# Hybrid decoder layer on one core: other chunks for the down projection, weights asked for in portions, a spread head, a convolution in steps and one load on another queue

## The chip, the cores and the metric

The kernel runs on one core of a Trainium2 chip. The metric is the device time of one launch in microseconds (us), median over the runs. A core has TensorE (PE, matrix products into PSUM), VectorE (DVE), ScalarE (ACT), GpSimd (POOL) and SyncE (SP); each works through its own instructions in order, and SP and POOL also issue DMA transfers, each in the order of its own queue.

## The reference

One decoder layer on an input `x` of 1024 positions by 1024 features, in float32, one sequence:

```python
x = x + 0.5 * swiglu(rms_norm(x, g1), gate1, up1, down1)          # d_ff = 2816
h = rms_norm(x, g_mix)
z = h @ w_in + b_in               # q, k, v of attention; q, k, v, gates of an mLSTM; two branch gates
y_attn  = sliding_window_attention(a_q, a_k, a_v, sinks) @ w_proj_attn      # 16 heads, window 128
qk      = silu(causal_depthwise_conv(concat(m_q, m_k), w_conv))             # width 4
y_mlstm = (sigmoid(m_o) * head_norm(mlstm(qk, m_v, m_i, m_f))) @ w_proj_mlstm
x = x + (sigmoid(g_a) * y_attn + sigmoid(g_m) * y_mlstm) @ w_out
x = x + 0.5 * swiglu(rms_norm(x, g2), gate2, up2, down2)
out = rms_norm(x, g_final)

def swiglu(x, gate, up, down): return (silu(x @ gate) * (x @ up)) @ down
def rms_norm(x, g): return x * rsqrt(mean(x * x) + 1e-6) * g
```

## The kernel before, in words

Positions lie along the free axis in two halves of 512, features along the partitions in eight tiles of 128, so `X[k][h]` is a tile of 128 x 512 in float32. Each float32 product is made of three TensorE matmuls: an operand is split into a high part, rounded for TensorE by a ScalarE copy, and a low part, the rest, by a VectorE subtraction (`parted`: lines 346 and 347). Then high times high, high times low and low times high are summed in PSUM.

**Feed-forward.** Both feed-forwards use a scheme of seven products for a 2 x 2 block product, numbered `PRODUCTS = 1, 2, 6, 7, 5, 4, 3`, with sums of weight blocks (`sum_of`) and sums of activation blocks (`mixed`) formed on VectorE beforehand. `gate_up` walks over eleven slices of the hidden features. Its `load` fetches a weight block of 128 x 1024 over SP's queue, `split` makes high and low parts, `product` does the matmuls (line 437), and `group` reads the result from PSUM (line 476 is ScalarE's copy for product 1). The first `LEAD` = 4 slices do products 1 and 2 ahead of the others, while the remaining operands are still being made; their blocks are loaded again for products 6 to 3, at fixed counts of `done` prepared units. The results are multiplied (`gated`), combined into the seven operands of the down product (`paired`) and stored to DRAM as the array `gd`.

The down stage, in `ffn`, cuts the eleven slices into chunks, `DOWN = ((0, 3), (3, 4), (7, 4))` as (first, count). Over each chunk it runs seven steps, one for each product, in the order `DOWN_ORDER = 1, 2, 6, 7, 4, 5, 3`. A step is four groups (`times`, matmuls at line 656) of 3 matmuls for each slice, 512 columns wide; the last step of the second feed-forward is done in two halves of 256 columns. What comes in:

- the chunk's weights, four blocks, over SP's queue (`load`): those of the first chunk all at product 2 of the last gate/up slice (`tail`), those of a later one in the chunk before;
- the step's operand from `gd`, over GpSimd's queue, three steps ahead (`fetch`): one in `tail` at product 7, three more at product 4, and from step 1 on one at each step;
- the rows of `x` to which the result is added (`loadx`, SP's queue): even tiles of the first half ahead of the first step, the rest in steps 1 to 3.

`prepare` makes high and low parts of the coming weights, two units a step, somewhat over one step ahead, and forms the weight sums behind them. Lines 688 to 694 are VectorE's additions of results to `u` and to the rows of `x`. The additions, the low parts and the sums stand in one order on VectorE.

**Head.** The kernel loads `x`, takes squares on ScalarE and adds them on VectorE (`stats`, lines 261 and 264; an addition is held back until the next square is issued), makes row sums with small matmuls against a constant (`rstd_rows`, line 272), the root on GpSimd, and spreads the row factor `r` over the partitions (`spread`, ScalarE copy at line 282). Before, all eight squares of the second half stand in ScalarE's order ahead of the copy of the first half's `r`; VectorE then normalises (line 752) and the products of the first gate/up stage start.

**Mix.** Each half goes through `mix`. Attention and mLSTM blocks are issued in a hand-made order, and between them `fill` takes steps of matrix products (`gemm`) from a list of tasks, as many as make up the time given. `ensure` runs tasks to their end where a result is needed. `gemm` hands its PSUM result to an evaluator; for the tiles of the convolution it is `ev_conv`, which does the four taps at once on VectorE (line 955) and defers only the silu (`later`: ScalarE's tanh at line 960, VectorE at line 961). `out_b` at line 1137 is the addition that makes an attention output, `ot`, from the PSUM tile `po`.

**Residual.** After the first half's mix, eight products with `w_out` are added to rows of `x` from DRAM (`xload` over SP's queue, two rows ahead, `ev_res` at line 1436), squared and summed. The norm of the second half runs beside it, its eight rows loaded over SP's queue just before.

**End.** The last step of the second feed-forward closes each tile with `done2`, and `final` multiplies the last quarter by its row factor (line 1550) and stores it.

Of the kernel before, what the change touches and what calls it, by code (L numbers as in the profile page):

```python
# [13 lines left out]
AF = mybir.ActivationFunctionType  # L14
# [5 lines left out]
KT = D // 128  # L20
# [3 lines left out]
HALVES = ((0, HS), (HS, HS))  # L24
QUARTERS = ((HS, HS // 2), (HS + HS // 2, HS // 2))
UNIT = D
DOWN = ((0, 3), (3, 4), (7, 4))
DOWN_ORDER = (1, 2, 6, 7, 4, 5, 3)
RING = 24
PRODUCTS = (1, 2, 6, 7, 5, 4, 3)  # L30
# [75 lines left out]
def layer(ctx, tc, I, out):  # L106
# [159 lines left out]
    def rstd_rows(psum, acc, v, n=4):  # L266

        flush()
        ps = psum.tile([128, n, 2], F32, name="mm")
        for b in range(n):  # L270
            for j, a in enumerate(acc):
                nc.tensor.matmul(ps[:, b], a[:, 128 * b:128 * b + 128], mean, start=j == 0, stop=j == len(acc) - 1)
        nc.vector.tensor_scalar(v, ps[:, :, 0], EPS, None, op0=OP.add)
        nc.gpsimd.tensor_tensor(v, v, mhalf[:, :n], op=OP.pow)

# [115 lines left out]
    def gate_up(n, pool, psum, op, gd, lead, tail, ahead):  # L391
# [131 lines left out]
        def prepare():  # L523

            nonlocal done
            nxt = next(rest, None)
            if nxt is None:
                yield from ahead()
                return
            lo = split(*nxt)  # L530
            yield
            lo()
            done += 1
            if done == 3:
                load(3, 0, 0), load(3, 0, 1)
                early.clear()
            elif done == 4:
                load(0, 1, 0), load(0, 1, 1)
            elif done == 7:
                load(0, 0, 1)  # L540
            elif done == 8:
                load(0, 0, 0), load(1, 0, 0)
                sum_of(0, 3), sum_of(0, 2)
            behind(*nxt)
            yield
# [17 lines left out]

    def ffn(n, pool, psum, op, gd, X, loadx, lead, done):

        steps = [(c, p) for c in range(len(DOWN)) for p in DOWN_ORDER]
        units = [(c, p, j) for c, p in steps for j in range(2)]
        last = len(DOWN) - 1
# [23 lines left out]

        def sum_of(c, j, i):
            w = 256 * DOWN[c][1]
            a, b, d, e = (raw[c, m, h][:, w * j:w * j + w] for m in range(2) for h in range(2))
            if i == 2:
                two_sum[c, j] = pool.tile([128, UNIT], F32, name="wr", bufs=4)[:, :w]
            t = two_sum.get((c, j))
            f, o, x, y = {3: (nc.vector.tensor_sub, a, a, d), 2: (nc.vector.tensor_sub, t, e, a),
                          1: (nc.vector.tensor_add, d, d, e), 4: (nc.vector.tensor_sub, b, b, t)}[i]  # L600
            f(o, x, y)

        def prepare():
            nonlocal ready
# [23 lines left out]
        def tail(p):  # L628
            if p == 2:
                for m in range(2):  # L630
                    for h in range(2):
                        load(0, m, h)
            elif p == 7:
                moving["buf", 0] = slot(1, [2, 4, 2, HS])
                fetch(0)
            elif p == 4:
                moving["buf", 1] = slot(2, [2, 4, 2, HS])
                for i in range(1, 4):
                    fetch(i)

        yield from gate_up(n, pool, psum, op, gd, lead, tail, prepare)
# [16 lines left out]
            return ps  # L658

        for i, (c, p) in enumerate(steps):  # L660
            if i:
                fetch(i + 3)
            if i == 1:
                for d in range(0, KT, 2):
                    loadx(d, 1)
# [40 lines left out]
    with ExitStack() as c1:  # L706
# [12 lines left out]
            nc.sync.dma_start(X[k][h], I["x"][h, :, k])  # L719

        def lead():
            yield from mixed(pool, X, 0, r1, op, own)
            bg.append(late_consts(pool))

        def warm(n):
# [10 lines left out]
        acc = [temp(pool) for h in range(2)]  # L736
        for k in range(KT):
            stats(pool, acc[0], X[k][0], k == 0)
        rs0, rs1 = (rstd_of(pool, psum, [a]) for a in acc)
        next(rs0)  # L740
        warm(12)
        for k in range(KT):
            stats(pool, acc[1], X[k][1], k == 0)
        for r in rs0:
            pass
        next(rs1)
        warm(4)
        next(f1)
        for k in range(KT + 1):
            o = op[1 + k // 4] if k < KT else None  # L750
            if k < KT:
                nc.vector.scalar_tensor_tensor(X[k][0], X[k][0], gains[:, 0, k:k + 1], r, op0=OP.mult, op1=OP.mult)
                nc.scalar.activation(o(k % 4, 0), X[k][0], AF.Copy)
            if k:
                j, o = k - 1, op[1 + (k - 1) // 4]
                nc.vector.tensor_sub(o(j % 4, 1), X[j][0], o(j % 4, 0).bitcast(F32))
            if k == 3:
                for r1 in rs1:
                    pass
        Hm = []  # L760

        def done1(d, p):
# [38 lines left out]
    def gemm(key, src, ev):  # L801
        hi, lo = W.get(key)
        ps = psum.tile([128, HS], F32, name="mm")
        for k in range(KT):
            mm3(ps, hi[:, k], lo[:, k], src[:, k, 0], src[:, k, 1], k == 0, k == KT - 1)
            if k == 3:
                W.mid()
            if k in (1, 3, 5):
                yield 1.3
        later = ev(ps)  # L810
        yield 1.3
        if later:
            deferred.append(later)


    deferred = []
# [1 line left out]
    def mix(hf, sH, sO, sQ, H, m0):  # L818
# [3 lines left out]
        def step():  # L822
            if state["cur"] is None:
                if not queue:
                    return None
                key, g = queue.pop(0)
                state["cur"] = (key, g)
            try:
                t = next(state["cur"][1])
                while t and deferred:  # L830
                    deferred.pop(0)()
                pump()
                return t
            except StopIteration:
                done.add(state["cur"][0])
                state["cur"] = None
                return 0.0
# [106 lines left out]
        def ev_conv(kind, t, dst):  # L944
            tile_ = (T_MQ if kind == 0 else T_MK) + t
            w = conv[:, 4 * kind + t]
            hs = hist[:, 4 * kind + t]

            def ev(ps):
                z = pool.tile([128, 3 + HS], F32, name="zb", bufs=1)  # L950
                nc.gpsimd.tensor_copy(z[:, :3], hs)
                nc.scalar.activation(z[:, 3:], ps, AF.Identity, bias=binf[:, tile_:tile_ + 1])
                nc.vector.tensor_scalar(dst, z[:, 0:HS], w[:, 0:1], None, op0=OP.mult)
                for j in range(1, 4):
                    nc.vector.scalar_tensor_tensor(dst, z[:, j:j + HS], w[:, j:j + 1], dst, op0=OP.mult, op1=OP.add)
                nc.gpsimd.tensor_copy(hs, z[:, HS:])

                def later():
                    th = z[:, :HS]
                    nc.scalar.activation(th, dst, AF.Tanh, scale=0.5)  # L960
                    nc.vector.scalar_tensor_tensor(dst, th, 1.0, dst, op0=OP.add, op1=OP.mult)
                return later
            return ev


# [452 lines left out]
    with ExitStack() as c3:  # L1418
# [10 lines left out]
        def xload(d):  # L1429
            if d < KT:  # L1430
                xr[d] = op.tile([128, HS], F32, name="xr", bufs=4)
                nc.sync.dma_start(xr[d], xd[0, :, d])

        def ev_res(d):
            def ev(ps):
# [189 lines left out]
```

## Time and profile before

| | |
|---|---|
| runs | 2423.58, 2416.15, 2421.65 us; median 2421.65 |
| profiled execution | 2410.58 us, its span 2408.4 us |
| mean granted TensorE clock | 0.988 |
| TensorE busy | 2341.1 us (97%), 11138 matmuls |
| VectorE busy | 1700.8 us (71%) |
| ScalarE busy | 971.1 us (40%) |
| GpSimd busy | 240.8 us (10%) |
| DMA | 361.46 MB, mean 150 GB/s |

The profile is of one execution, with times counted from its first instruction. Busy times are sums over an engine's instructions; waits are the idle time of an engine ahead of an instruction, put down to the work that ended last before it. L437 is line 437 of the kernel. The granted clock is a share of TensorE's full clock.

### The profile page before, as it was taken

To read this page: it belongs to the slowest core of one execution; us is meant where nothing else is said; L and a number is where in the kernel's file an instruction comes from. 1 tells how busy PE (TensorE), PEld (TensorE's weight loads), DVE (VectorE), ACT (ScalarE), POOL (GpSimd) and SP (SyncE) were. 2 spreads that over 40 slices of the span, in tenths; PEclk is the share of its full clock that TensorE was granted. 3 is DMA by queue.
4 is the path that set the end of the run, shared out by engine and by line. 5 is a ranking of instruction groups with operands and counts; after the bars stand their busy time and mean duration, and the time that the engine had idled before them with its cause. 6 is when DMAs were issued, how large, how long until landed. Compare 5 with 4: busy or idle time off the path is not lost.

```text
span 2408.4 us, 30172 instructions
## 1 busy us (share of the span) xinstructions
PE 2341.1 (97%) x11138; PEld 1947.2 (81%) x11138; DVE 1700.8 (71%) x2720; ACT 971.1 (40%) x1728; POOL 240.8 (10%) x242
## 2 busy tenths in 40 slices
PE   8999999999999999999999999999999999999997
PEld 7788888878887878888777878888888888887886
DVE  7998877866667754555567754554689988887766
ACT  5434343322247742333347742333353433332223
POOL 0000000000034220100044220100000000000000
PEclk9999999999999999999999999999999999999999
DMA  4464543998431223222532223222545645359862
GB/s 171 130 203 166 164 148 133 337 334 281 166 106 53 75 64 99 69 80 84 176 94 60 67 66 98 66 82 88 183 147 162 200 147 182 124 206 393 281 212 104
DMA packets 154324, 361.46 MB, mean 150 GB/s; under 512 B 13504, under 2 KB 22848, under 8 KB 154176
## 3 DMA queue, kind: packets, MB, share of 16 engines
q1 hardware_dynamic: 131728, 277.79, 35.4%
q0 software_dynamic: 21584, 81.53, 9.8%
q8 instruction: 88, 1.44, 0.2%
q14 instruction: 60, 0.49, 0.1%
q10 hardware_dynamic: 864, 0.21, 0.1%
HBM read 263.27 MB, written 96.21 MB: 149 GB/s over the span
## 4 chain that ended last, share of the span: by engine, by line
PE 77%; DVE 11%; DMA 6%; ACT 3%; issue 2%; SPq 0%; POOL 0%; DVEq 0%; ACTq 0%
PE mm L437 30%; PE mm L656 13%; PE mm L327 8%; PE mm L329 8%; PE mm L328 8%; DMA gd<-nsq 2%; PE mm L936 1%; PE mm L937 1%; PE mm L938 1%; DMA nsq<-x 1%; DMA s<-dn 1%; DVE wlo L347 1%; ACT P L1085 1%; DVE P L1075 1%; PE lm L1220 1%
## 5 line engine op out<-in xcount | busy, mean ns | idle before, releaser
L437 PE MATMUL mm<-s,whi 128*128 128x512 f32 x2112 | 653.7, 391 | 5.4 <-ACT nsq L476 4.9
L437 PEld LDWEIGHTS mm<-s,whi 128*128 128x128 f32 x2112 | 397.7, 188 | 90.5 <-ACT nsq L476 5.8
L327 PE MATMUL mm<-s,whi 128*128 128x512 f32 x1056 | 422.9, 400 | 0.9 <-DVE s L1405 0.9
L329 PE MATMUL mm<-s,wlo 128*128 128x512 f32 x1056 | 414.7, 393 | 1.5 <-POOL wlo L88 1.5
L328 PE MATMUL mm<-s,whi 128*128 128x512 f32 x1056 | 413.8, 392 | 0.0
L437 PE MATMUL mm<-s,wlo 128*128 128x512 f32 x1056 | 412.1, 390 | 0.0
L656 PE MATMUL mm<-s,whi 128*128 128x512 f32 (+1 forms) x1264 | 385.6, 387 | 2.8 <-DVE nsq L694 1.5
L656 PEld LDWEIGHTS mm<-s,whi 128*128 128x128 f32 x1264 | 237.1, 190 | 51.8 <-DVE nsq L694 2.4
L656 PE MATMUL mm<-s,wlo 128*128 128x512 f32 (+1 forms) x632 | 245.0, 388 | 7.3 <-DVE wlo L347 7.3
L329 PEld LDWEIGHTS mm<-s,wlo 128*128 128x128 f32 x1056 | 199.5, 189 | 46.5 <-POOL wlo L88 3.2
L327 PEld LDWEIGHTS mm<-s,whi 128*128 128x128 f32 x1056 | 199.9, 189 | 42.4 <-issue 4.1
L437 PEld LDWEIGHTS mm<-s,wlo 128*128 128x128 f32 x1056 | 198.9, 188 | 41.1 <-DVE wlo L347 0.2
L328 PEld LDWEIGHTS mm<-s,whi 128*128 128x128 f32 x1056 | 199.9, 189 | 37.5
L88 DVE TENSOR_TENSOR wlo<-wraw,whi 128x1024 fp32r<-128x1024 f32 (+1 forms) x138 | 174.6, 1265 | 68.1 <-ACT whi L76 67.7
L76 ACT ACTIVATE whi<-wraw 128x1024 fp32r<-128x1024 f32 (+1 forms) x154 | 159.4, 1042 | 68.8 <-DMA wraw<-win 19.7
L346 ACT ACTIVATE whi<-wr 128x1024 fp32r<-128x1024 f32 (+1 forms) x122 | 127.9, 1049 | 100.2 <-DVE wr L427 50.2
L346 ACT ACTIVATE whi<-s 128x1024 fp32r<-128x1024 f32 (+1 forms) x72 | 70.9, 987 | 211.5 <-PE mm L656 191.8
L347 DVE TENSOR_TENSOR wlo<-wr,whi 128x1024 fp32r<-128x1024 f32 (+1 forms) x122 | 147.5, 1209 | 8.1 <-ACT whi L346 8.0
L346 ACT ACTIVATE nsq<-nsq 128x512 fp32r<-128x512 f32 x162 | 98.9, 624 | 134.3 <-DVE nsq L347 55.4
L656 PEld LDWEIGHTS mm<-s,wlo 128*128 128x128 f32 x632 | 119.9, 190 | 32.6 <-DVE wlo L347 9.0
L590 POOL DMA_DIRECT2D s<-gd x42 | 31.9, 760 | 1109.5 <-DMA s<-dn 439.3
L485 DVE TENSOR_TENSOR nsq<-mm,nsq 128x512 f32<-128x512 f32 x132 | 90.4, 685 | 59.1 <-PE mm L437 59.0
(277 smaller groups left out, 3452.8 us busy)
## 6 DMA issues: line engine op xcount, KB each, us to landing
gd<-nsq SPq DMA_DIRECT2D x308, 256.0 KB, 4.4
s<-gd POOLq DMA_DIRECT2D x28, 2048.0 KB, 8.4
wraw<-win SPq DMA_DIRECT2D x84, 512.0 KB, 3.6
wr<-gu SPq DMA_DIRECT2D x74, 512.0 KB, 4.6
s<-gd POOLq DMA_DIRECT2D x14, 1536.0 KB, 12.7
s<-dn SPq DMA_DIRECT2D x16, 1024.0 KB, 9.7
wraw<-gu SPq DMA_DIRECT2D x30, 512.0 KB, 4.2
nsq<-x SPq DMA_DIRECT2D x32, 256.0 KB, 7.2
```

The lines of the kernel that those rows point to most:

```text
L76: self.nc.scalar.activation(hv, v, AF.Copy)
L88: (self.nc.gpsimd if self.on_pool else self.nc.vector).tensor_sub(lv, v, hv.bitcast(F32))
L327: nc.tensor.matmul(ps, hi, xh, start=first, stop=False)
L328: nc.tensor.matmul(ps, hi, xl, start=False, stop=False)
L329: nc.tensor.matmul(ps, lo, xh, start=False, stop=last)
L346: nc.scalar.activation(hi, x, AF.Copy)
L347: return lambda: nc.vector.tensor_sub(lo, x, hi.bitcast(F32))
L437: nc.tensor.matmul(ps, a[:, k], op[p](k, x), start=first and k == 0 and j == 0, stop=k == 3 and j == 2, skip_group_check=not first)
L485: nc.vector.tensor_add(st[s, to, w], ps, st[s, key, w])
L590: nc.gpsimd.dma_start(t, gd[PRODUCTS.index(p), s0:s0 + a].rearrange("s p i t -> p s i t"))
L656: nc.tensor.matmul(ps, wt[:, f], t[:, f, x, c], start=first and f == 0 and q == 0, stop=f == a - 1 and q == 2, skip_group_check=not first)
L936: nc.tensor.matmul(ps, x[:, 0], hi, start=k == 0, stop=False)
```

## The change

- The down stage's chunks become 4, 3, 4 slices in the first feed-forward and 4, 4, 3 in the second. The first chunk's four weight blocks are asked for at products 2 (two), 6 and 5 of the last gate/up slice. `fetch` runs at every step from step 0 on, with two instead of three in `tail` at product 4. `sum_of` in the down stage picks its blocks only as it uses them.
- In `gate_up`, block `(0, 0, 0)` is loaded again after six prepared units instead of eight.
- In the head, the first weights' parts are made earlier; two squares of the second half stand ahead of the copy of `r`, the other six stand between the normalising steps, each in a tile of its own, and are not added on VectorE: `rstd_rows` sums the seven tiles on TensorE, with its loops exchanged. The second half's `r` is waited for in `lead`.
- A convolution's three later taps and its last multiply become four deferred steps, one at each step of the list of tasks; an evaluator of a convolution first runs all that is still deferred. The tanh is issued behind the third tap.
- `xload` issues over GpSimd's queue.

```diff
-DOWN = ((0, 3), (3, 4), (7, 4))
+CHUNKS = {1: ((0, 4), (4, 3), (7, 4)), 2: ((0, 4), (4, 4), (8, 3))}
...
         ps = psum.tile([128, n, 2], F32, name="mm")
-        for b in range(n):
-            for j, a in enumerate(acc):
-                nc.tensor.matmul(ps[:, b], a[:, 128 * b:128 * b + 128], mean, start=j == 0, stop=j == len(acc) - 1)
+        for j, a in enumerate(acc):
+            for b in range(n):
+                nc.tensor.matmul(ps[:, b], a[:, 128 * b:128 * b + 128], mean, start=j == b == 0,
+                                 stop=j == len(acc) - 1 and b == n - 1, skip_group_check=True)
...
             elif done == 4:
                 load(0, 1, 0), load(0, 1, 1)
+            elif done == 6:
+                load(0, 0, 0)
             elif done == 7:
                 load(0, 0, 1)
             elif done == 8:
-                load(0, 0, 0), load(1, 0, 0)
+                load(1, 0, 0)
                 sum_of(0, 3), sum_of(0, 2)
...
         def tail(p):
             if p == 2:
                 for m in range(2):
-                    for h in range(2):
-                        load(0, m, h)
+                    load(0, m, 0)
+            elif p == 6:
+                load(0, 1, 1)
+            elif p == 5:
+                load(0, 0, 1)
             elif p == 7:
                 moving["buf", 0] = slot(1, [2, 4, 2, HS])
                 fetch(0)
             elif p == 4:
                 moving["buf", 1] = slot(2, [2, 4, 2, HS])
-                for i in range(1, 4):
+                for i in range(1, 3):
                     fetch(i)
...
         for i, (c, p) in enumerate(steps):
-            if i:
-                fetch(i + 3)
+            fetch(i + 3)
...
         def lead():
-            yield from mixed(pool, X, 0, r1, op, own)
+            for r in rs1:
+                yield
+            yield from mixed(pool, X, 0, r, op, own)
...
-        rs0, rs1 = (rstd_of(pool, psum, [a]) for a in acc)
+        rs0 = rstd_of(pool, psum, [acc[0]])
         next(rs0)
-        warm(12)
-        for k in range(KT):
+        warm(4)
+        next(f1)
+        for k in range(2):
             stats(pool, acc[1], X[k][1], k == 0)
+        flush()
         for r in rs0:
             pass
-        next(rs1)
-        warm(4)
-        next(f1)
+        warm(8)
+        squares = [acc[1]]
+        rs1 = rstd_of(pool, psum, squares)
         for k in range(KT + 1):
...
-            if k == 3:
-                for r1 in rs1:
-                    pass
+            if k < KT - 2:
+                squares.append(temp(pool))
+                nc.scalar.activation(squares[-1], X[2 + k][1], AF.Square)
+            elif k == KT - 2:
+                next(rs1)
...
         later = ev(ps)
         yield 1.3
-        if later:
-            deferred.append(later)
+        deferred.extend(later or [])
...
-                while t and deferred:
+                if t and deferred:
                     deferred.pop(0)()
...
             def ev(ps):
+                while deferred:
+                    deferred.pop(0)()
                 z = pool.tile([128, 3 + HS], F32, name="zb", bufs=1)
...
-                for j in range(1, 4):
+
+                def tap(j):
                     nc.vector.scalar_tensor_tensor(dst, z[:, j:j + HS], w[:, j:j + 1], dst, op0=OP.mult, op1=OP.add)
-                nc.gpsimd.tensor_copy(hs, z[:, HS:])
-
-                def later():
-                    th = z[:, :HS]
-                    nc.scalar.activation(th, dst, AF.Tanh, scale=0.5)
-                    nc.vector.scalar_tensor_tensor(dst, th, 1.0, dst, op0=OP.add, op1=OP.mult)
-                return later
+                    if j == 3:
+                        nc.gpsimd.tensor_copy(hs, z[:, HS:])
+                        nc.scalar.activation(z[:, :HS], dst, AF.Tanh, scale=0.5)
+
+                def last():
+                    nc.vector.scalar_tensor_tensor(dst, z[:, :HS], 1.0, dst, op0=OP.add, op1=OP.mult)
+                return [lambda j=j: tap(j) for j in range(1, 4)] + [last]
...
                 xr[d] = op.tile([128, HS], F32, name="xr", bufs=4)
-                nc.sync.dma_start(xr[d], xd[0, :, d])
+                nc.gpsimd.dma_start(xr[d], xd[0, :, d])
```

## Rows read from the trace of the kernel before

**Rows 1.** The page: span, and busy time, share and instructions of each engine.
```profile
span 2408.4 us, 30172 instructions
...
PE 2341.1 (97%) x11138; PEld 1947.2 (81%) x11138; DVE 1700.8 (71%) x2720; ACT 971.1 (40%) x1728; POOL 240.8 (10%) x242
```

**Rows 2.** Waits of PE: instruction <- releaser: total us, times, longest us.
```profile
PE mm L656 <- DVE wlo L347: 7.3, 4, 2.2
...
PE mm L437 <- ACT nsq L476: 4.9, 2, 4.8
...
PE po L1126 <- DVE ot L1137: 4.3, 4, 2.0
PE mm L272 <- DVE nacc L264: 3.9, 1, 3.9
```

**Rows 3.** Stretches: us; PE, PEld, DVE, ACT, POOL busy; granted clock; DMA share; GB/s.
```profile
200.00:400.00 200.00, 200.00 (x884) 165.67 (x883) 164.35 (x214) 79.69 (x107) 0.00 (x0) 1.00 0.49 158
60.00:80.00 20.00, 15.25 (x62) 12.06 (x61) 18.50 (x25) 13.23 (x23) 0.35 (x1) 0.91 0.25 74
430.00:490.00 60.00, 60.00 (x266) 49.71 (x265) 47.08 (x66) 20.29 (x30) 6.38 (x8) 1.00 1.07 381
485.00:525.00 40.00, 34.77 (x142) 27.28 (x141) 28.02 (x39) 7.38 (x8) 3.00 (x4) 0.96 1.07 387
845.00:865.00 20.00, 17.48 (x82) 13.91 (x81) 15.90 (x29) 12.34 (x29) 9.31 (x12) 0.91 0.18 55
...
2200.00:2240.00 40.00, 35.13 (x145) 27.68 (x144) 28.86 (x40) 7.71 (x9) 3.00 (x4) 0.96 1.08 392
```

**Rows 4.** Timeline of the head: start us, us, engine, line, op, count, [idle <- releaser].
```profile
12.36 0.95 PE L272 MATMUL mm<-mean,nsq 128*128 128x2 f32 x8
...
19.66 0.58 ACT L282 ACTIVATE nsq<-mm 128x512 f32<-128x512 f32 x1
20.95 1.84 PE L272 MATMUL mm<-mean,nsq 128*128 128x2 f32 x8 [4.42 <-DVE nsq L264]
...
25.19 1.40 DVE L752 SCALAR_TENSOR_TENSOR nsq<-nsq,gains 128x512 f32<-128x512 f32 x2
...
26.64 1.52 PE L437 MATMUL mm<-s,whi 128*128 128x512 f32 x2 [0.47 <-ACT s L753]
```

**Rows 5.** Timeline of the first gate/up stage, VectorE and ScalarE near 70 us.
```profile
68.51 1.23 DVE L427 TENSOR_TENSOR wraw<-wraw,wr 128x1024 f32<-128x1024 f32 x1 [1.03 <-DMA wraw<-gu]
...
71.03 1.06 ACT L346 ACTIVATE whi<-wr 128x1024 fp32r<-128x1024 f32 x1 [6.77 <-DVE wr L427]
```

**Rows 6.** Timeline of the first down stage: its first matmul, and VectorE at 492 us.
```profile
454.88 0.62 PE L656 MATMUL mm<-s,whi 128*128 128x512 f32 x2
...
492.16 0.69 DVE L690 TENSOR_TENSOR nsq<-nsq 128x512 f32<-128x512 f32 x1 [4.92 <-DMA nsq<-x]
492.77 0.95 DVE L347 TENSOR_TENSOR wlo<-s,whi 128x768 fp32r<-128x768 f32 x1
```

**Rows 7.** Timeline of VectorE at the end of the first attention stage.
```profile
853.35 3.48 DVE L955 SCALAR_TENSOR_TENSOR lq<-zb,conv,lq 128x512 f32<-128x512 f32 x3
...
857.61 0.69 DVE L961 SCALAR_TENSOR_TENSOR lq<-zb,lq 128x512 f32<-128x512 f32 x1 [0.78 <-ACT zb L960]
858.23 0.68 DVE L1137 TENSOR_TENSOR ot<-po,ot 64x512 f32<-64x512 f32 x1
```

**Rows 8.** Timeline of VectorE in the residual stage.
```profile
1173.60 0.69 DVE L1436 SCALAR_TENSOR_TENSOR xr<-mm,xr 128x512 f32<-128x512 f32 x1 [5.12 <-DMA xr<-xd]
...
1190.06 0.68 DVE L1436 SCALAR_TENSOR_TENSOR xr<-mm,xr 128x512 f32<-128x512 f32 x1
...
1192.11 0.68 DVE L264 TENSOR_TENSOR nacc<-nacc,nsq 128x512 f32<-128x512 f32 x1
```

**Rows 9.** Timeline of VectorE in the tail: first final multiply, last addition of results.
```profile
2385.78 0.75 DVE L1550 SCALAR_TENSOR_TENSOR nsq<-nsq,gains 128x512 f32<-128x512 f32 x1 [1.18 <-ACT nsq L282]
...
2394.16 0.42 DVE L694 TENSOR_TENSOR nsq<-mm,nsq 128x256 f32<-128x256 f32 x1
```

More of the change, by code (lines that the diff above doesn't have):

```diff
@@ L564, in ffn @@
     def ffn(n, pool, psum, op, gd, X, loadx, lead, done):
+        DOWN = CHUNKS[n]
         steps = [(c, p) for c in range(len(DOWN)) for p in DOWN_ORDER]
@@ L594, in sum_of, with at @@
             w = 256 * DOWN[c][1]
-            a, b, d, e = (raw[c, m, h][:, w * j:w * j + w] for m in range(2) for h in range(2))
+            def at(m, h):
+                return two_sum[c, j] if m == 2 else raw[c, m, h][:, w * j:w * j + w]
             if i == 2:
                 two_sum[c, j] = pool.tile([128, UNIT], F32, name="wr", bufs=4)[:, :w]
[L598 to L601, printed above, removed]
+            f, o, x, y = {3: (nc.vector.tensor_sub, (0, 0), (0, 0), (1, 0)), 2: (nc.vector.tensor_sub, (2, 0), (1, 1), (0, 0)),
+                          1: (nc.vector.tensor_add, (1, 0), (1, 0), (1, 1)), 4: (nc.vector.tensor_sub, (0, 1), (0, 1), (2, 0))}[i]
+            f(at(*o), at(*x), at(*y))
         def prepare():
```

## The prediction

> **What bounds the kernel now.** The page comes first: TensorE's matmuls are busy 97% of a span of 2408.4 us [rows 1]. No other engine is near that on average, so only stretches in which TensorE stands still, or runs at half clock, can be won. A busy matmul row doesn't show throughput, so the table by stretches is read next, for counts: in 200 us without a stall it has 884 matmuls of 512 columns, 0.2262 us each [rows 3]. Any other stretch of such matmuls has lost its length minus count times 0.2262:
> - 60 to 80 us, first gate/up stage: 62 matmuls are 14.0 us of work, **6.0 us lost** [rows 3].
> - 485 to 525 us, first down stage: 142 are 32.1 us, **7.9 us lost** [rows 3].
> - 2200 to 2240 us, second down stage: 145 are 32.8 us, **7.2 us lost** [rows 3].
>
> The ends of the two attention stages have small shapes too, so there idle time and clock are read: 17.48 us busy of 20 (2.5 us idle) at a mean granted clock of 0.91, that is 1.8 us more at the lower of the two levels, **4.3 us** [rows 3]. The row of the second, 1390 to 1410 us, has the same two numbers, so 8.6 us together.
>
> The list of TensorE's waits says who ended them [rows 2]: the down stages wait for the low parts of weights from VectorE (7.3 us), the gate/up stage for a PSUM copy by ScalarE (4.8 us), attention for VectorE's `ot` (4.3 us), and the residual stage once for the last add of squares (3.9 us). The timeline then shows what is late behind each of them. All of these are places that the diff touches.
>
> **Part 1, head and first gate/up stage.** Before, VectorE starts normalising the first half at 25.19 us, since ScalarE's copy of the first `r` (19.66) stands behind all squares of the second half, and VectorE first adds seven of these [rows 4]. Now ScalarE does two squares ahead of that copy and VectorE one add; six adds (0.68 us each, as the L264 row shows [rows 8]) become row sums on TensorE. I work out VectorE's new order: the first half's row sums are done at 13.3 us as before [rows 4], two low parts of weights (1.23 us each, as the L427 row, which has their operation and shape [rows 5]) and one add bring 16.6 or somewhat later, then come eight steps of a multiply and a low part, 0.7 us each [rows 4], against a start at 25.19. But the second half's row sums grow from 8 to 56 small matmuls, and stand in TensorE's order ahead of the first product. Eight of them took 1.84 us at 20.95, after an idle gap, and 0.95 us at 12.36, behind the warm-up [rows 4]. 56 at the first rate are 12.9 us and, from about 17.4 us (16.6 and a square), end at 28.5 to 30 us; at the second they are 6.7 us, so they follow ScalarE's squares and end near 26. So the first product starts between 26.5 and 30 us against 26.64 [rows 4], and VectorE, which has one row-sum result in its loop to wait for, is 4.9 to 7.5 us ahead of before. I take the slow side, since the new ones too come piecemeal behind squares, with gaps: start +0.7 us, VectorE 4.9 us ahead.
>
> Of the clock in this head the rows show 8 row-sum records in 1.84 us after an idle gap of 4.42 us [rows 4]. The Trainium skill ("TensorE: Matmul & The Clock Gate", Part 1) says that an idle engine drops to half rate and that sustained activity releases it; were the row sums to count as activity, the products would start at full rate and part 1 would give some 3 us more, which is inside the range below.
>
> The 6.0 us at 60 to 80: TensorE waits for the ScalarE copy at L476, which is queued behind a weight copy that sat 6.77 us until VectorE had formed a weight sum (L427), which itself had waited only 1.03 us for the reload of `(0, 0, 0)` [rows 5]. So earlier loading alone buys 1.0 us; the rest of the stall is VectorE's lateness. With both, the copy comes 4.9 + 1.0 = 5.9 us earlier, which is more than the wait of 4.8 [rows 2]; the stall goes. Part 1: -6.0 + 0.7 = **-5.3** (from -9, fast row sums, to -1, if VectorE's lead is used up). In the second feed-forward the same earlier load meets no wait of TensorE: 0.
>
> **Part 2, down chunks and portioned loads.** In 430 to 490 us the DMA engines move 381 GB/s at a share over 1 [rows 3]: full. VectorE's residual add at L690 waits 4.92 us for a reloaded row of `x`, the low part of a weight is queued behind it (492.77), and TensorE waits for that [rows 6]. The chunk starts at 454.88 [rows 6]. A step has 36 matmuls with 3 tiles, 48 with 4: 8.14 or 10.86 us. That add belongs to step 3 after its first 9 (12) matmuls: due at 481.3 before, landed 492.1, so 10.8 us late, and the weight behind it is due at step 4's half, 454.9 + 4.5 x 8.14 = 491.5. Now the add is due at 490.2 and the weight at 503.8. Bytes up to that row, by the shapes: before 4 x 0.79 (weights) + 24 x 0.26 (products' rows) + 7 x 1.57 (fetches) + 9 x 0.26 (`x`) = 22.7 MB from 430 to 492, in fair agreement with the 381 GB/s. Now 4 x 1.05 + 6.3 + 6 x 2.1 + 2.4 = 25.5 MB, 67 us at 381: landing at 497. Plus an add and a low part (0.69 + 1.2) the weight is ready at 499, 5 us in hand. So the loss goes, in both feed-forwards. The upper bound is 7.9 + 7.2 = 15.1; I leave 3 us for what remains, more in the second, whose next chunk is 4 tiles too and so loads 4.2 MB instead of 3.1: **-12** (-15 to 0). The portions: the last of the first four weights is now asked for after product 5, two products (2 x 24 x 0.2262 = 10.9 us) ahead of the first step; if it is late by a few us, ScalarE waits, and it is busy 40% [rows 1].
>
> The price is at the end: the second feed-forward's last chunk now has 3 tiles. VectorE works from 2385.78 to 2394.58 (8.8 us) without a gap, on adds and on eight final multiplies [rows 9], past the last matmul. In the last step TensorE has 72 instead of 96 half-width matmuls, 24 x 0.113 (half of 0.2262) = 2.7 us less cover, and the multiplies start 1 us earlier, as the groups ahead of them are shorter: **+2** (0 to +4).
>
> **Part 3, convolution in steps.** VectorE does three taps in one piece of 3.48 us, then waits for ScalarE's tanh, then does L961 at 857.61, and only then the `ot` that TensorE waits for [rows 7]. Spread over steps of the filler, one tap of 1.16 us stands ahead of `ot`, which can start at 853.35 + 1.16 = 854.5 instead of 858.23; as the longest of the four waits for it was 2.0 us [rows 2], 856.2 is soon enough. The stall goes at the end of both attention stages; later heads are pulled in by an ensure that runs all taps at once, as before, and TensorE isn't short there. Of 8.6 us I take **-6.5** (-8.6 to -2).
>
> **Part 4, residual rows on GpSimd's queue.** The first row stood on the SP queue behind eight loads, and VectorE waited 5.12 us for it [rows 8]. That delay mostly heals by itself: the last add of squares ends at 1192.79, and TensorE's wait of 3.9 us [rows 2] with it, so the product ahead ended at 1188.9, and the chain of the last rows starts at 1190.06, only 1.1 us behind it [rows 8]. So -1 (-1.5 to 0). GpSimd's queue then holds eight DMA issues ahead of or between the norm's work; the waits of the last four are for stores two steps old. The Trainium skill ("Trainium Kernel Development and Optimization", Key Constraints) says that all queues share the same DMA engines and another issuer only saves issue time; by it this part would give 0, and the 5.12 us agree only in that they were order, not bandwidth.
>
> **Sum**: -5.3 - 12 + 2 - 6.5 - 1 = -22.8. The profiled execution took 2410.58 us (2.2 around its span), so the new one should take about 2388. The median of the runs shown is 2421.65, 11 us above the profiled one; taking the same difference, the forecast is 2421.65 - 22.8 = **2399**.
>
> **The rivals.**
> - *The row of transfers still ends the down stages.* If SP's queue is served a third of the rate while fetches are pending, the row of `x` lands a few us later than 499, and the later ones and the next chunk's weights too. For: the engines stay full, and fetches are a third larger. Against: 5 us in hand. Part 2 then gives -3 instead of -12: 2408.
> - *Row sums and spread taps don't pay.* VectorE stays as late at the first weight sum, or `ot` stays behind two taps: parts 1 and 3 at their poor ends, +4.3 and +4.5: also 2408.
> - *All stalls go and the row sums are quick*: -9 - 15 - 8.6 - 1.5 + 1 = -33: 2389.
> - *Slower: fetches late.* Four fetches of 2.1 MB instead of 1.57 are asked for around the start of each down stage. If they are served behind the weights, each step's operand lands after its step begins. The second fetch must land within 15.7 us of its issue at about 450; 2.1 MB at a third of 381 GB/s is 16.5 us a fetch, against a step of 10.86: 5.7 us lost a step, over six steps in two stages +68, and 2421.65 - 10.8 + 68 = 2479. It decides from 2 us a step (24 us). Against it: no wait of TensorE for a fetch among the first ones listed, in stages already full.
>
> **Chances.** Forecast (2394 to 2405): 0.45. All go (below 2394): 0.16. The two partial cases (2405 to 2414): 0.21. Within 0.3% (7 us, about what a measurement here can tell from nothing): 0.10, where both partial cases come together. Slower: 0.08. So faster 0.82. The range from 2387 to 2415 leaves 3% below and 15% above; the likeliest case's own range is 2394 to 2405.
>
> **What would show it.** Right: in the first down stage no wait of TensorE for L347's low parts; 62 matmuls in 60 to 80 us become about 88; `ot` no longer follows a tap block; granted clock 1.0 through both attention ends; the last VectorE multiplies end later after the last matmul. Wrong: TensorE waiting on a fetch or on L347 in steps 3 to 6, a first product later than 30 us, or a tail longer by over 4 us.

## The result and the profile after

The changed kernel takes **2388.24 us** (median of 4 runs, 2387.03 to 2388.59) against 2420.9 us of the kernel before (4 runs, 2416.15 to 2423.58): a ratio of 0.9866 with a 95% interval of 0.9849 to 0.9883, or 32.7 us less. The forecast was 2399 in a range of 2387 to 2415. The two profiled executions differ by less: their spans are 2408.4 and 2386.8 us, 21.6 apart, where the sum of the prediction said 22.8. So there are two questions: whether the terms of the sum are right, and where the other 11 us come from.

Line numbers below are those of each kernel itself; the changed one's are 1 to 15 higher (L437 is L438, L656 is L664, L1137 is L1152). The page of the changed kernel, span and busy times (beside [rows 1]):

```profile
span 2386.8 us, 30232 instructions
...
PE 2337.4 (98%) x11166; PEld 1948.9 (82%) x11166; DVE 1692.9 (71%) x2714; ACT 969.0 (41%) x1728; POOL 237.9 (10%) x250
```

TensorE's waits, beside [rows 2] (in us in total, times, longest):

```profile
PE mm L281 <- POOL nv L275: 6.5, 3, 4.0
...
PE mm L438 <- DVE nsq L486: 3.4, 4, 1.4
...
PE mm L272 <- DVE nacc L264: 2.8, 1, 2.8
PE mm L664 <- DVE wlo L348: 2.7, 2, 2.1
```

The wait for the ScalarE copy and the wait of `po` for `ot` are gone from the list. The low parts of the down weights fell from 7.3 to 2.7 us. L438's waits for VectorE's addition at L486 grew (the kernel before had one of 1.4 us), and the longest in total is now L281's for GpSimd's root (4.8 us before).

The table by stretches, with the columns of [rows 3]:

```profile
60.00:80.00 20.00, 20.00 (x90) 16.57 (x89) 17.73 (x23) 12.09 (x20) 0.35 (x1) 1.00 0.26 71
430.00:490.00 60.00, 60.00 (x266) 49.67 (x266) 46.93 (x61) 20.26 (x28) 5.42 (x7) 1.00 1.09 397
485.00:525.00 40.00, 37.89 (x168) 31.05 (x167) 28.82 (x39) 6.52 (x8) 2.48 (x4) 1.00 1.03 369
...
840.00:865.00 25.00, 25.00 (x161) 21.82 (x160) 20.36 (x28) 13.79 (x30) 10.01 (x14) 1.00 0.28 90
1380.00:1405.00 25.00, 25.00 (x160) 21.59 (x158) 19.98 (x27) 12.67 (x24) 9.15 (x13) 1.00 0.29 91
2190.00:2230.00 40.00, 39.41 (x175) 32.29 (x174) 27.75 (x37) 7.43 (x7) 2.24 (x3) 1.00 1.09 398
```

60 to 80 us now holds 90 matmuls instead of 62, 485 to 525 us 168 instead of 142, and both attention ends run without a gap at a granted clock of 1.00. The DMA engines are as full as before.

Matching the same matmul in both traces (the k-th of its line) gives the shift, and its steps are the terms of the sum:

```
first product of the first gate/up stage     +1.2
76 us                                        -5.8
end of the first gate/up stage               -3.5   (+2.3 near 125 and 154 us)
end of the first down stage                  -9.1   (-5.6)
ahead of / behind the first attention end    -8.7 / -13.2   (-4.5)
behind the residual stage                   -13.7   (-0.5)
ahead of / behind the second attention end  -14.5 / -18.8   (-4.3)
end of the second gate/up stage             -17.7   (+1.1)
second down stage, ahead of its last step   -24.5   (-6.7)
end of the span                             -21.7   (+2.8)
```

The 76 us are of the kernel before, the 125 and 154 us of the changed one. The spans as the pages print them differ by 21.6. The shift ahead of the last step is that of its last matmul which both kernels do 512 columns wide: in the last step itself the k-th matmul is no longer the same, since the changed kernel has 12 wide matmuls more ahead of it and 24 half-width ones fewer in it.

The head, in the timeline (beside [rows 4]) and then by stretches:

```profile
16.62 1.41 DVE L763 SCALAR_TENSOR_TENSOR nsq<-nsq,gains 128x512 f32<-128x512 f32 x2 [0.97 <-ACT nsq L283]
...
18.62 9.37 PE L272 MATMUL mm<-mean,nsq 128*128 128x2 f32 x56
...
27.85 1.20 PE L438 MATMUL mm<-s,whi 128*128 128x512 f32 x2
```
```profile
18.60:21.40 2.80, 2.80 (x28) 2.80 (x26) 2.80 (x6) 2.71 (x6) 0.00 (x0) 1.00 1.05 408
21.40:24.00 2.60, 2.60 (x14) 2.60 (x14) 2.60 (x5) 2.37 (x5) 0.00 (x0) 0.51 0.69 265
24.00:27.80 3.80, 3.80 (x19) 3.80 (x20) 1.08 (x2) 1.03 (x2) 0.00 (x0) 0.50 0.00 2
27.80:31.40 3.60, 3.60 (x9) 2.84 (x10) 3.02 (x5) 2.52 (x3) 1.45 (x1) 0.50 0.00 0
```

VectorE starts at 16.62 as worked out, and the 56 row sums take 9.37 us, between the two prices. These were prices of the two clock levels: in the kernel before, the granted clock was 1.00 from 12 to 15 us and 0.50 from 21 to 24 us. The row sums stand without a gap, yet the granted clock falls to the lower level, 1.2 GHz, at 21.4 us in their middle, and the first products run at it.

VectorE where the down stage still waits (beside [rows 6]), and at the first attention end (beside [rows 7]):

```profile
491.16 0.68 DVE L695 TENSOR_TENSOR nsq<-mm,nsq 128x512 f32<-128x512 f32 x1
501.17 0.69 DVE L697 TENSOR_TENSOR nsq<-nsq 128x512 f32<-128x512 f32 x1 [9.33 <-DMA nsq<-x]
501.78 1.22 DVE L348 TENSOR_TENSOR wlo<-s,whi 128x1024 fp32r<-128x1024 f32 x1
...
```
```profile
849.86 1.52 DVE L970 SCALAR_TENSOR_TENSOR lq<-zb,conv,lq 128x512 f32<-128x512 f32 x2
852.77 0.69 DVE L1152 TENSOR_TENSOR ot<-po,ot 64x512 f32<-64x512 f32 x1 [1.38 <-ACT ot L1147]
853.48 0.69 DVE L976 SCALAR_TENSOR_TENSOR lq<-zb,lq 128x512 f32<-128x512 f32 x1
```

In the down stage VectorE stands idle for 9.33 us behind L695 until a row of `x` lands, and the low part that TensorE needs is queued behind the addition at L697. At the attention end two taps are done by 851.4 us, `ot` waits for ScalarE alone, and the last multiply L976 comes after it; TensorE has other work meanwhile.

### The profile page after: what moved, and what is told of

Its sections match the earlier page's. It is cut to its first block, busy times and chain, and to the rows that moved or that the text cites. A ratio compares the mean times of both kernels' runs of the same rounds, so it can differ in the third digit from the quotient of the medians.

```text
span 2386.8 us, 30232 instructions
## 1 busy us (share of the span) xinstructions
PE 2337.4 (98%) x11166; PEld 1948.9 (82%) x11166; DVE 1692.9 (71%) x2714; ACT 969.0 (41%) x1728; POOL 237.9 (10%) x250
## 5 line engine op out<-in xcount | busy, mean ns | idle before, releaser
L438 PE MATMUL mm<-s,whi 128*128 128x512 f32 x2112 | 651.8, 390 | 0.0
L438 PEld LDWEIGHTS mm<-s,whi 128*128 128x128 f32 x2112 | 397.1, 188 | 82.5
L438 PE MATMUL mm<-s,wlo 128*128 128x512 f32 x1056 | 411.4, 390 | 0.0
L664 PE MATMUL mm<-s,whi 128*128 128x512 f32 (+1 forms) x1256 | 382.2, 386 | 0.0
L664 PEld LDWEIGHTS mm<-s,whi 128*128 128x128 f32 x1256 | 234.7, 188 | 47.2
L664 PE MATMUL mm<-s,wlo 128*128 128x512 f32 (+1 forms) x628 | 242.5, 386 | 2.7 <-DVE wlo L348 2.7
L438 PEld LDWEIGHTS mm<-s,wlo 128*128 128x128 f32 x1056 | 198.6, 188 | 41.3
L664 PEld LDWEIGHTS mm<-s,wlo 128*128 128x128 f32 x628 | 118.4, 188 | 27.3 <-DVE wlo L348 3.5
L486 DVE TENSOR_TENSOR nsq<-mm,nsq 128x512 f32<-128x512 f32 x132 | 90.5, 686 | 59.8 <-PE mm L438 59.8
```

The costliest lines, as they stand in the source:

```text
L438: nc.tensor.matmul(ps, a[:, k], op[p](k, x), start=first and k == 0 and j == 0, stop=k == 3 and j == 2, skip_group_check=not first)
L486: nc.vector.tensor_add(st[s, to, w], ps, st[s, key, w])
L664: nc.tensor.matmul(ps, wt[:, f], t[:, f, x, c], start=first and f == 0 and q == 0, stop=f == a - 1 and q == 2, skip_group_check=not first)
```

## The experiments

Times are medians of 4 to 12 runs beside the kernel before on the same chip (2420.7 to 2421.8 us there). Lost time of a stretch is its length minus 0.2262 us for each matmul in it.

**1. The kernel before again.** No edit.

> The kernel before, unchanged, to see what its executions have in common. Theory A: the 11 us by which the change gained more (32.7) than the spans of the two profiled executions differ (21.6) lie in the down stages of the kernel before, whose late transfers cost more in most executions than in the one that was profiled: runs spread over 4 us or more, and a profile with a longer span has it between 485 and 525 and between 2200 and 2240 us. Theory B: the whole execution is longer by a like amount everywhere (a clock, a chip): a longer span is spread over the stages. Theory C: the head, whose first loads wait for DMA, varies: the first product starts later than 26.6 us by the difference.

2419.77 us (2411.23 to 2424.68, 12 runs), ratio 0.9991 (0.9978 to 1.0004). The spread is 13 us. The execution that was profiled is, like the first one, among the shortest (2411.72), and its down stages lose 7.4 and 6.3 us:

```profile
485.00:525.00 40.00, 35.00 (x144) 27.53 (x143) 27.87 (x38) 7.86 (x9) 3.01 (x4) 0.96 1.08 388
2190.00:2240.00 50.00, 45.93 (x193) 36.55 (x192) 34.20 (x47) 11.43 (x13) 4.56 (x6) 0.97 1.08 397
```

**2. Down stages alone**, on the kernel before.

```diff
+CHUNKS = {1: ((0, 4), (4, 3), (7, 4)), 2: ((0, 4), (4, 4), (8, 3))}
...     with the portions in tail, fetch(i + 3) from step 0 on, sum_of's choice of blocks
```

> The kernel before with the chunks, the portioned loads and the earlier operand loads of the down stages alone. By the profiles of before and after, the down stages give back 5.7 and 7.5 us and the tail costs some 3.5: -10 us. Theory A: -20 us and runs within 2 us of each other, since what varies is gone. Theories B and C: -10 us and the spread of before.

2402.6 us (2401.35 to 2405.19), ratio 0.9924 (0.9911 to 0.9938): 19 us less, near theory A's 20, with a spread of 4 us where it said 2.

**3. The changed kernel with the old down stages.** The same edit taken back.

> The changed kernel with chunks and loads of its down stages as before. By the profiles: 2388 + 10 = 2398. Theory A: about 2408, spread over 4 us or more. Theories B and C: about 2398, runs within 2 us where the head or the clock was the cause.

2404.19 us (2400.14 to 2410.44), ratio 0.9932 (0.9915 to 0.9949): 16 us over the changed kernel where the spans gave 10, spread over 10 us; the time lies between A's 2408 and the others' 2398, the spread is A's. In its profile the second down stage loses 14.3 us, twice what [rows 3] shows:

```profile
485.00:525.00 40.00, 35.34 (x146) 27.85 (x145) 29.95 (x38) 8.68 (x10) 2.29 (x4) 0.96 1.04 378
2190.00:2240.00 50.00, 39.48 (x158) 30.98 (x157) 30.20 (x38) 9.70 (x12) 2.99 (x5) 0.93 0.84 303
```

**4. Head alone**, on the kernel before.

```diff
+            elif done == 6:
+                load(0, 0, 0)
...     with the order of squares, the seven tiles in rstd_rows, and lead as in the change
```

> The kernel before with the new head and the earlier reload of block (0, 0, 0) alone. By the profiles -3.5 us after what VectorE gives back at 125 and 154 us, and in the second feed-forward none. Theories A and B: -3.5 us. Theory C: -13 us or so, with a small spread.

2411.56 us (2406.05 to 2417.42), ratio 0.9961 (0.9948 to 0.9974): 10 us less, more than theories A and B said and less than C's 13, with a spread of 11 us where C said a small one. Its profiled execution lies at the median, and there the down stages, which it doesn't touch, lose 12.2 and 9.3 us:

```profile
485.00:525.00 40.00, 31.86 (x123) 24.82 (x122) 26.61 (x35) 6.53 (x7) 2.58 (x4) 0.91 0.94 340
2190.00:2240.00 50.00, 42.65 (x180) 34.44 (x179) 34.27 (x48) 10.95 (x13) 3.78 (x5) 0.97 1.06 384
```

**5. Convolution alone**, on the kernel before: `ev_conv`'s taps and last multiply deferred one at a step.

```diff
-                while t and deferred:
+                if t and deferred:
...
+                return [lambda j=j: tap(j) for j in range(1, 4)] + [last]
```

> The kernel before with the convolution in steps alone. By the profiles of before and after, whose shift against each other grows by 4.5 and 4.3 us at the ends of the two attention stages and by 0.4 near 720 us: -9 us against before, with the spread of before, as its down stages stay. Rival: the stall only moves to another wait for VectorE in the same stage, and the gain is under 4 us.

2407.4 us (2406.34 to 2412.09), ratio 0.9954 (0.9942 to 0.9966): 8 to 14 us less, with a spread of 6 us. The 9 lie inside; the rival's under 4 doesn't. In its profile the wait for `ot` falls from 4.3 to 0.4 us, so the cause is the one forecast. Its old down stages lose 13.3 and 6.6 us there (118 and 192 matmuls in the two stretches); up to the first of them its code is that of the kernel before.

**6. and 7. Other chunks**, on the changed kernel.

```diff
-CHUNKS = {1: ((0, 4), (4, 3), (7, 4)), 2: ((0, 4), (4, 4), (8, 3))}
+CHUNKS = {1: ((0, 4), (4, 4), (8, 3)), 2: ((0, 4), (4, 4), (8, 3))}     # 6
+CHUNKS = {1: ((0, 4), (4, 3), (7, 4)), 2: ((0, 4), (4, 3), (7, 4))}     # 7
```

> The changed kernel with 4, 4, 3 in the first feed-forward too. The changed kernel still lost 1.9 us between 485 and 525 us, in chunk 4, 3, 4, and the second feed-forward with 4, 4, 3 only 0.6: if the larger second chunk is what gives the transfers time, -1 to -2 us, about 2386.5. Rival: the second chunk's larger fetches and weights (4.2 MB instead of 3.1) are late in turn: 0 or slower.

> The changed kernel with 4, 3, 4 in the second feed-forward too. The tail after the last matmul is then 16.8 us again instead of 18.8, and its last step is longer by 24 short matmuls; the price is a stall like that of the first feed-forward, about 2 us at the second chunk: -1 us, no clear difference. Rival: the tail's price in the changed kernel is the whole 3.7 us by which the shift fell from the last step on, and the stall stays under 1 us: -3 us.

4, 4, 3 in both: 2388.83 us (2387.64 to 2390.02), ratio 0.9873 (0.9860 to 0.9886). The stretch from 485 us loses 0.9 instead of 2.0 us (173 matmuls), but the way from the last down product to the mix is 1.9 us longer: no gain. 4, 3, 4 in both: 2384.53 us (2383.32 to 2392.06), ratio 0.9862 (0.9845 to 0.9878). The time behind the start of the last matmul is 17.1 instead of 18.9 us, and the second down stage has no stall:

```profile
485.00:525.00 40.00, 36.52 (x151) 29.66 (x150) 27.41 (x37) 6.45 (x7) 2.73 (x4) 0.91 0.97 349
2190.00:2240.00 50.00, 49.80 (x220) 40.89 (x220) 36.66 (x49) 8.78 (x10) 3.79 (x5) 1.00 0.95 337
```

That agrees with the rival's 3 us, but the interval also holds the changed kernel's 0.9866. The first stretch, whose code is that of the changed kernel, lost 5.8 us here, in the longest of its four runs.

**8. Low parts stored over GpSimd's queue.**

```diff
                 for i in range(2):
-                    nc.sync.dma_start(gd[PRODUCTS.index(p), s, :, i], part[i].bitcast(F32))
+                    q = nc.gpsimd if i and s < 8 else nc.sync
+                    q.dma_start(gd[PRODUCTS.index(p), s, :, i], part[i].bitcast(F32))
```

> The changed kernel with the stores of the low parts of the first eight slices' down operands on GpSimd's queue. The changed kernel lost 2.3 us near 125 and 154 us and some 2 us in the second feed-forward, where TensorE waits for VectorE, which had waited 3.2 us for a store to land that stood behind weight loads on SP's queue. If it is that order: -2 to -4 us. Rival: the stores compete for the same DMA engines and land as late: 0.

2392.12 us (2390.74 to 2393.97), ratio 0.9889 (0.9874 to 0.9904): no gain. VectorE still waits for a store at the same place, 4.38 instead of 3.15 us. It came 1.4 us earlier, and the store, now on GpSimd's queue, landed at 114.85 instead of 115.03 us, 5.15 us behind its issue instead of 4.82. So the rival's result holds here; that the shared DMA engines are the reason isn't shown. Over the whole kernel the 112 stores on GpSimd's queue landed in 3.3 us (median), the 196 left on SP's in 4.9, against 4.4 for all 308 of the changed kernel. First the changed kernel, then this one:

```profile
115.15 0.69 DVE L348 TENSOR_TENSOR nsq<-nsq 128x512 fp32r<-128x512 f32 x1 [3.15 <-DMA gd<-nsq]
```
```profile
114.98 0.70 DVE L348 TENSOR_TENSOR nsq<-nsq 128x512 fp32r<-128x512 f32 x1 [4.38 <-DMA gd<-nsq]
```

**9. and 10. Odd rows of `x` a step earlier**, on the changed kernel and on number 7.

```diff
-            elif i in (2, 3):
+            if i in (1, 2):
                 for d in range(1, KT, 2):
-                    loadx(d, i - 2)
+                    loadx(d, i - 1)
```

> The changed kernel with the odd rows of x asked for one step earlier (first half at step 1, second half at step 2), so ahead of six stores on SP's queue. In the changed kernel VectorE waited 9.3 us for the first of them, landed at 501.1 us, and TensorE 2.1 us for the low part behind it. If the order on SP's queue is what holds that row: it lands by 495, the stall near 500 us goes, -2 to -4 us by the clock behind it, and an execution's down stages vary less. Rival: what sets the landing is the bandwidth shared with the fetches, and the fetches or the stores are late in turn: 0.

> The same on top of 4, 3, 4 in both feed-forwards, which ran at 2384.5 us with a stall of 3.5 us near 502 us in its profile and one execution of 2392. If the row of x is what was late there: -2 to -4 us, 2381 to 2383, runs within 3 us. Rival: 2384.5 and the same spread.

2390.68 us (2389.69 to 2397.82), ratio 0.9885 (0.9865 to 0.9905), and 2387.17 us (2382.69 to 2389.05), ratio 0.9865 (0.9844 to 0.9886). The row is issued at 477.88 us instead of 487.35 and lands at 490.6 instead of 501.1, and the stretch from 485 us holds 176 matmuls: that stall is gone. In the changed kernel SP issued each transfer from 474 to 494 us as the one eight places ahead of it landed (the row's issue at 487.35 behind a landing at 487.33), so the order on SP's queue held the row. But a new stall of 3.0 us ends at 481.9, where the low part of a down operand waits for a tile that a store still holds, with the low part of a weight (480.65) queued behind it:

```profile
473.15 0.68 DVE L701 TENSOR_TENSOR nsq<-mm,nsq 128x512 f32<-128x512 f32 x1
480.04 0.69 DVE L348 TENSOR_TENSOR nsq<-nsq 128x512 fp32r<-128x512 f32 x1 [6.21 <-DMA gd<-nsq]
480.65 1.22 DVE L348 TENSOR_TENSOR wlo<-wr,whi 128x1024 fp32r<-128x1024 f32 x1
...
481.92 0.50 PE L664 MATMUL mm<-s,wlo 128*128 128x512 f32 x1 [3.01 <-DVE wlo L348]
```

What was expected of the row is right, and the rival decides the time; the runs spread over 8 and 6 us, so they don't vary less either.

**11. Without portions**, on the changed kernel.

```diff
-                    load(0, m, 0)
-            elif p == 6:
-                load(0, 1, 1)
-            elif p == 5:
-                load(0, 0, 1)
+                    for h in range(2):
+                        load(0, m, h)
```

> The changed kernel with the first chunk's four weight blocks all asked for at product 2 of the last slice, as before. If the chunks are what removed the stalls of the down stages: no difference (within 3 us). Rival: the portions matter, since four blocks of 1 MB at once delay the stores ahead of the first fetch and the rows of x: +4 us or more.

2387.21 us (2384.52 to 2393.88), ratio 0.9871 (0.9850 to 0.9892): no difference. The profile shows an exchange. Neither down stage loses anything in its stretch, but TensorE's waits for L486 grew from 3.4 to 8.7 us, among them 1.4 and 2.4 us at the ends of the two gate/up stages:

```profile
485.00:525.00 40.00, 40.00 (x178) 33.14 (x177) 30.36 (x40) 7.01 (x7) 3.01 (x4) 1.00 1.04 372
2190.00:2240.00 50.00, 50.00 (x223) 41.40 (x222) 36.51 (x46) 10.16 (x10) 3.72 (x5) 1.00 1.01 366
```
```profile
PE mm L438 <- DVE nsq L486: 8.7, 7, 2.4
```

So the chunks, with the earlier `fetch`, remove the stalls of the down stages without the portions. That the portions only choose where a smaller stall stands rests on this one execution.

**12. Residual rows on SP's queue again.**

```diff
-                nc.gpsimd.dma_start(xr[d], xd[0, :, d])
+                nc.sync.dma_start(xr[d], xd[0, :, d])
```

> The changed kernel with the residual stage's rows on SP's queue again. The wait for the last addition of squares was 3.9 us in the kernel before and is 2.8 in the changed one: +1 us, not to be told from nothing, with 3.9 us of that wait in the profile. Rival: the queue is worth the first row's whole wait: +4 us. Second rival: the shorter wait comes from elsewhere, and it stays 2.8.

2392.82 us (2385.67 to 2394.49), ratio 0.9883 (0.9861 to 0.9906), not told apart by its time. The profile tells it apart: the wait is 4.9 us instead of 2.8. It is 2.8 in all eight profiles with these rows on GpSimd's queue and 3.3 to 4.9 in the six with them on SP's:

```profile
PE mm L272 <- DVE nacc L264: 4.9, 1, 4.9
```

## Why the prediction was right, and where it was off

**Against the profiled execution the sum held**: 21.6 us measured, 22.8 forecast. In part that is luck: the head gave 2.9 us less than forecast and the tail cost 0.8 more, the convolution gave 2.3 us more. The terms:

- *Head* (-5.3): -3.5. The stall at 67 us goes, and the first product starts 1.2 us later (0.7 forecast). What failed is that VectorE's lead would last: at 115 us VectorE waits 3.15 us for a store to land, as it did in the kernel before (3.0), only there TensorE's own stall of 5 us had let it catch up. 2.3 us come back near 125 and 154 us. In the second gate/up stage waits for the same line (L486) cost 1.1 where I had put 0.
- *Down stages* (-12): -5.6 and -6.7, together -12.3. The row of `x` was forecast at 497 us and landed at 501.1, so the 5 us in hand became a wait of 2.1 in step 4, one of the prediction's own signs of being wrong. The size fits only because I had left 3 us for what remains. I had counted bytes only; experiment 9 shows that its place on SP's queue, behind stores, set the landing. So the first rival's mechanism was there too, at some 2.5 us in the two stretches instead of its 9.
- *Tail* (+2): +2.8. Behind the last matmul it is 2 as forecast; the other 0.8 is inside the last step, where TensorE now waits 0.7 us for VectorE's sum of squares (L264). The expectations above that speak of 3.5 or 3.7 us here, and of 7.5 in the second down stage, each took some 0.8 us too much.
- *Convolution* (-6.5): -8.8 at the two ends. I had kept 2.1 us back for a remainder, and there is none at the ends. The table's +0.4 near 720 us and -0.8 behind the residual stage belong to no term.
- *Residual rows* (-1): -0.5 in the shift. The wait itself fell from 3.9 to 2.8, and experiment 12 takes it to 4.9. The Trainium skill ("Trainium Kernel Development and Optimization", Key Constraints) lets another issuer save issue time alone. The measurement differs: 2.8 against 4.9 us, with the same bytes. On SP's queue (number 12) the first row was issued at 1155.3 us, behind eight loads, on GpSimd's at 1100.4.

The clock in the head was the other open point. The Trainium skill ("TensorE: Matmul & The Clock Gate", Part 1) has activity release the throttle; the row sums ran without a gap and the clock fell to 0.51 in their middle, so the 3 us more didn't come.

**The step that failed is the last one**: "taking the same difference", by which 11 us between the median and the profiled execution were carried over to the changed kernel. They weren't there: its profiled execution took 2388.59 us, with the median at 2388.24. The kernel before had been profiled twice, both times in one of its shortest executions. Lost time in the two stretches of the down stages, by counts of matmuls in the profiles:

```
                              first   second   sum (us)
before, before again        7.9, 7.4  7.2, 6.3  15.1, 13.7
head alone                      12.2     9.3      21.5
convolution alone               13.3     6.6      19.9
changed, old down stages         7.0    14.3      21.3
down stages alone                5.6     1.1       6.7
changed                          2.0     0.5       2.5
```

The table also rests on these lines, in this order: the kernel before (second stretch), convolution alone (both), down stages alone (both) and the changed kernel (second). The last line is that of number 12 (first stretch), for what is said below.

```profile
2190.00:2240.00 50.00, 45.13 (x189) 35.97 (x188) 35.42 (x48) 9.98 (x12) 3.77 (x5) 0.97 1.08 393
485.00:525.00 40.00, 30.92 (x118) 24.01 (x117) 24.36 (x34) 5.82 (x7) 2.26 (x3) 0.88 0.98 360
2190.00:2240.00 50.00, 46.15 (x192) 36.70 (x192) 36.45 (x48) 10.87 (x13) 3.78 (x5) 0.97 1.08 391
485.00:525.00 40.00, 35.91 (x152) 29.23 (x151) 26.40 (x36) 6.16 (x6) 2.25 (x3) 0.96 0.99 356
2190.00:2240.00 50.00, 48.95 (x216) 40.25 (x215) 37.72 (x50) 11.55 (x12) 3.72 (x5) 1.00 1.09 398
2190.00:2240.00 50.00, 49.41 (x219) 40.58 (x218) 35.87 (x46) 10.70 (x12) 2.98 (x4) 1.00 1.04 377
485.00:525.00 40.00, 36.53 (x154) 29.75 (x153) 29.37 (x39) 5.94 (x6) 2.27 (x3) 0.96 0.94 337
```

So the old down stages lose between 14 and 21 us, from one execution to the next, and the two profiles of the kernel before lie at the low end. By the middle three, which are other kernels with the same down stages, I estimate that a usual execution loses some 6 us more there than I read from [rows 3]. Exchanging the down stages alone was worth 19 and 16 us in experiments 2 and 3, against 12.3 less the tail's 2.8 in the profiled pair. That much is shown. The changed down stage of the first feed-forward varies too: with the same code it lost 2.0 us in the changed kernel, 5.6 in number 2, 5.8 in number 7 and 5.2 in number 12, so the changed kernel's 2.0 is a low sample as well.

That the remaining 5 us of the 11 are the same thing is only argued: no execution of the kernel before near 2421 us has a trace here. What is on record speaks against the two other theories of number 1. For a clock: the execution profiled there had a mean granted clock of 0.986, as had three others of that run which took 2419.6 to 2421.7 us. For the head: in the four profiles with the old head the first down stage starts between 454.3 and 456.1 us, and one of them is the longest run of number 2. It also stays open why the parts don't add up: taken alone they give 19, 10 and 13 us, in sum 42, and all together give 33. One reading is that each of them moves the down stages to a better or worse moment.

Of the rivals, *all stalls go* named the time (2389) but not the reason: stalls remain, and row sums at 9.37 us aren't quick. *Fetches late* found nothing: no wait of TensorE for a fetch is in the list, and the fetch for step 1 of the first down stage landed at 459.0 us, 3.2 us ahead of that step.

No version tried is clearly faster than the changed kernel. 4, 3, 4 in both feed-forwards has the lowest median, 2384.5, inside the interval.

## What to carry to other kernels

A stall that is read from one profiled execution is one sample, and here the stages in which transfers fill the DMA engines varied most: ask how that execution stands to the median before carrying the difference over, and profile it a second time. A stall removed upstream gives back what another engine had caught up in it; look for the next wait of that engine (here it took back 2.3 of 5.8 us). Bytes alone don't date a transfer: count what stands ahead of it on its own queue, and which buffer its new place takes.

## What the runs showed that was not expected

- TensorE's granted clock fell from 1.00 to 0.51 at 21.4 us during 56 row sums that stood without a gap, and was 0.50 for the first products up to 31.4 us.
- The store that VectorE waits for at 115 us landed as late over GpSimd's queue as over SP's, 5.15 us behind its issue instead of 4.82, and splitting the stores over two queues took nothing off the time.
- The same old down stages lost 7.0 to 13.3 us in the first stretch and 6.3 to 14.3 in the second, over five executions.
